# Four accumulator banks in turn for the mLSTM projections and gate tiles, and two accumulators for the modulation sums, in a one-core hybrid layer kernel

## The chip, the cores and the metric

The kernel runs on one core of a Trainium2 chip. The metric is the device time in microseconds from launch to end. TensorE does the matrix products and writes into PSUM, which has eight banks of 128 x 512 float32; VectorE (DVE), ScalarE (ACT) and GpSimd (POOL) do the elementwise work, and SyncE (SP), ScalarE and GpSimd issue DMA transfers. A PSUM bank can be given to a new product only when everything that reads the old one is done.

## The reference

One layer over 1024 latent tokens and 256 context tokens, width 1024. Cut to what matters:

```
u    = x * (1 + scale) + shift                       # latent; the context tokens likewise
p    = u @ w_in + b_in                               # 9280 columns, cut into q, k, v, gates ...
q, k = silu(short_conv(concat(q_m, k_m), conv_qk))   # mLSTM, 8 heads of 128: taps t-1, t, t+1
h_m  = mLSTM scan, both directions                   # chunked, with log-sum-exp gates
h_g  = gated linear attention (GLA), 4 heads, both directions
mix  = (sigmoid(gate_a) * (norm(h_m) * sigmoid(o_m)) @ w_branch_mlstm
        + sigmoid(gate_b) * (norm(h_g) * silu(z_g)) @ w_branch_gla) @ w_out
h    = layer_norm(ALPHA * h + g1 * mix)
h    = layer_norm(ALPHA * h + g2 * conv_glu(h * (1 + sc2) + sh2))
```

The vectors shift, scale, g1, sh2, sc2 and g2 are `silu(c) @ w_mod + b_mod`, 6144 columns. The first 2048 are made at the start; the other 4096 are made beside the GLA branch projection.

## The kernel before

Every large product is done as three products of rounded float32 halves (`mm3`, lines 279 to 285: high by high on L283, high by low on L284, low by high on L285). A **block** is one output tile of 128 x 512: 8 steps over the inner dimension by 3 products, so 24 matmuls into one PSUM bank. A block over the 256 context tokens has 24 matmuls of half the width.

**PSUM** is one pool with four tags of two banks each: `pj`, `pa`, `po` and `pt`. A tile of a tag takes one of its two banks as soon as that bank's last reader is done.

**The order on each engine** is not the order of the program text. A planner takes the instructions with their place in the text as their priority and lays out a fixed list for each engine, by its own costs; an instruction whose bank or buffer it holds to be taken yields to a later one. So the lists of TensorE, VectorE, ScalarE, GpSimd and the DMA queues are fixed when the kernel is made, and on the chip each engine goes through its list in order, with waits.

**The mLSTM stage.** For each head h, in the order of the text: the projections of q and k of head h+1 (`ml_proj_qk`, five blocks: two for q over the latent tokens, called q0 and q1 here, and three for k, called k0, k1 and the short k2 over the context); for every second head the projection of v for two heads (`ml_proj_v`, 240 half-width matmuls, always in `pj`); the last transposes of the head before (`late`, L844, evacuated by ScalarE on L845); the scan of head h (`ml_scan`); and one or two gate tiles (`fill`, `gate_tile`, two blocks each). TensorE fills the pauses of the scan with blocks of gate tiles. All blocks of q, k and the gate tiles lie in `pj`.

A block of q or k is read from its bank by one ScalarE instruction (L732) and by two to four VectorE instructions after it (the taps on L727, a one-column copy on L737, and edge columns). A gate tile's block is read by one ScalarE instruction (L537), which then goes out by a DMA of ScalarE's queue.

Inside `ml_scan`, GpSimd issues the loads of the decay tiles (L760, L761 and L764), ScalarE takes exponentials of them (L765, L769), and the products of k and q (L786, two tiles of four chunks) lie in `pa`. The GLA scan's last outputs lie in `pa` too, two tiles that are read on L690.

**The GLA branch stage.** For each of eight column blocks j of the branch output: `mod_sum(j)` adds up eight slices of `w_mod`, scaled by silu(c), into an accumulator on VectorE (L908), after a memset on GpSimd (L901) and a small DMA of the bias (L903). Four loads of 512 KB feed it through two buffers (L906). Then come two blocks of the branch product (mm3 on L956, banks `pj`, `pa`, `po` in turn), each scaled by a gate tile that is loaded (L953), passed through tanh (L954), multiplied (L957) and stored (L958). Then `mod_row(j)` sums the accumulator over its 128 partitions with a matmul (L913), copies the row (L914) and stores it (L915). All eight accumulators are the same buffer, `u19`.

Of the kernel before, what the change touches and what calls it, by code (L numbers as in the profile page):

```python
# [15 lines left out]
P = 128  # L16
# [20 lines left out]
def layer_kernel(ctx, tc, I, out, dbg=None):  # L37
# [16 lines left out]
    def nm(s):  # L54
        cnt[0] += 1
        return f"{s}_{cnt[0]}"

    def pt(tag, shape):
        return ps.tile(shape, F32, tag=tag, name=nm(tag))
# [17 lines left out]
    def ubt(i, shape, dt=F32):  # L77
        return ub.tile(shape, dt, tag=f"u{i}", name=nm(f"u{i}"))
# [35 lines left out]
    for l in range(7):  # L114
        h = 1 << l
# [47 lines left out]
    for k in range(KD):  # L163
        for hf in range(2):
            w = ubt(2 * k + hf, [P, 1024])
# [28 lines left out]
    for k in range(KD):  # L194
# [3 lines left out]
        for i in range(2):  # L198
            w = wm[2 * k + 1][:, 512:1024]
# [7 lines left out]
    for i in range(2):  # L207
        hi = stg.tile([P, 2, 256], F32R, tag="whi", name=nm("whi"), bufs=6)
        lo = stg.tile([P, 2, 256], F32R, tag="wlo", name=nm("wlo"), bufs=6)
        h, l = (t[:].rearrange("p a (b c) -> p (a b) c", c=P) for t in (hi, lo))  # L210
# [99 lines left out]
    def u_blk(b):  # L310
        if b < 2:
            return lambda k: (uh[k][:, b * 512:b * 512 + 512], ul[k][:, b * 512:b * 512 + 512])
        return lambda k: (cuh[k // 4][:, k % 4, :], cul[k // 4][:, k % 4, :])
# [9 lines left out]
    def proj(w, c, b, tag="pj"):  # L323
        p = pt(tag, [P, 512])
        mm3(p[:, 0:BW[b]], lambda k: w(k, c, P), u_blk(b))
        return p
# [68 lines left out]
    p = proj(w0, P, 2)  # L395
# [6 lines left out]
    for d, n in enumerate(("gla_gate_w_fwd", "gla_gate_w_bwd")):  # L402
# [4 lines left out]
        w = slot(10 + d, [96, SEQ], F32R)[:, 0:512]  # L407
# [121 lines left out]
            parts.append((hi, lo))  # L529
        return lambda k, c, n: tuple(t[:, k % 4, c:c + n] for t in parts[k // 4])  # L530

    def gate_tile(dst, off, cb0, j):
        w = wtile(w_in, off + j * P)
        for b in range(2):
            p = proj(w, 0, b)
            t = sc.tile([P, 512], F32, tag="gt", name=nm("gt"), bufs=2)
            A.activation(t[:], p[:], AF.Identity, scale=0.5, bias=cB(cb0 + j))  # L537
            A.dma_start(dst[j][:, b * 512:b * 512 + 512], t[:])
# [178 lines left out]
    def ml_proj_qk(h):  # L717
        w = wload([(w_in, O_QM + h * P, P, 0), (w_in, O_KM + h * P, P, P)])
        res = []
        for i in range(2):  # L720
            n = SEQ if i == 0 else L
            y = slot((0, 4)[h % 2] + i, [P, n])
            t0, t1, t2 = (cB(c_cv + 16 * j + 8 * i + h) for j in range(3))
            bs, b0, b2 = (cvb[:, j, 8 * i + h:8 * i + h + 1] for j in range(3))

            def tap(o, src, t):
                V.scalar_tensor_tensor(y[:, o:o + src.shape[1]], src, t, y[:, o:o + src.shape[1]],  # L727
                                       op0=ALU.mult, op1=ALU.add)
            for b in range(2 + i):
                m, o = BW[b], b * 512  # L730
                p = proj(w, i * P, b)
                A.activation(y[:, o:o + m], p[:, 0:m], AF.Identity, scale=t1, bias=bs)  # L732
                tap(o + 1, p[:, 0:m - 1], t0)
                tap(o, p[:, 1:m], t2)
                if b == 0:
                    ed = sc.tile([P, 1], F32, tag="ed", name=nm("ed"), bufs=2)
                    V.tensor_copy(ed[:], p[:, m - 1:m])  # L737
                if b == 1:
                    tap(o, ed[:], t0)
                    tap(o - 1, p[:, 0:1], t2)  # L740

                if b != 1:
                    V.tensor_tensor(y[:, o:o + 1], y[:, o:o + 1], b0, op=ALU.subtract)  # L743
                if b != 0:
                    V.tensor_tensor(y[:, o + m - 1:o + m], y[:, o + m - 1:o + m], b2, op=ALU.subtract)
            th = slot(15, [P, n])
            A.activation(th[:], y[:], AF.Tanh, scale=1.0 / QS if i == 0 else 1.0)
            V.scalar_tensor_tensor(y[:], th[:], 1.0, y[:], op0=ALU.add, op1=ALU.mult)
            res.append(y)
        return res  # L750
# [104 lines left out]

    gates = [(thb_d, O_GB, c_gb, j) for j in range(8)] + [(tha_d, O_GA, c_ga, j) for j in range(8)]

    def fill(n):
        for _ in range(n):
            gate_tile(*gates.pop(0))  # L860

    for h in range(GH):
        q, k = gla_qk(h) if h else (q0, k0)
# [13 lines left out]
    for h in range(MH):  # L877
        nxt = ml_proj_qk(h + 1) if h + 1 < MH else None
        if h and h % 2 == 0:
            v2 = ml_proj_v(h // 2)  # L880
        late()
        rest.append(ml_scan(h, *qk, v2[h % 2]))
        qk = nxt
        fill(2 if h < 2 or h > 5 else 1)
    late()
    while gates:
        fill(1)
# [4 lines left out]
    tags = ("pj", "pa", "po")  # L892
# [4 lines left out]
        return tags[seq[0] % 3]  # L897

    def mod_sum(b):
        acc = ubt(19, [P, 512])  # L900
        G.memset(acc[:], 0.0)  # L901
        c0 = 2048 + b * 512
        SY.dma_start(acc[0:1, :], I["b_mod"][c0:c0 + 512].unsqueeze(0))  # L903
        for k2 in range(0, KD, 2):
            raw = ubt((16, 18)[k2 // 2 % 2], [P, 2, 512])
            SY.dma_start(raw[:], I["w_mod"][k2 * P:(k2 + 2) * P, c0:c0 + 512].rearrange("(k p) c -> p k c", p=P))  # L906
            for i in range(2):
                V.scalar_tensor_tensor(acc[:], raw[:, i, :], sC[:, k2 + i, 0:1], acc[:], op0=ALU.mult, op1=ALU.add)  # L908
        return acc

    def mod_row(b, acc):
        p = pt("pt", [P, 512])
        T.matmul(p[0:1, :], ones[:], acc[:], start=True, stop=True)  # L913
        V.tensor_copy(acc[0:1, :], p[0:1, :])  # L914
        SY.dma_start(md_d[b * 512:b * 512 + 512].unsqueeze(0), acc[0:1, :])  # L915

    def gated(off, cb0, src_d, silu):
        hi, lo = [], []
        for j2 in range(4):
            w = wload([(w_in, off + j2 * 256, 256, 0)])  # L920
            for e in range(2):
                j = 2 * j2 + e
                hi.append(slot(j, [P, SEQ], F32R))
                lo.append(slot(8 + j, [P, SEQ], F32R))
                hr = ubt(16 + j % 2, [P, SEQ])
                SY.dma_start(hr[:], src_d[j][:])
                ht = ubt(18, [P, SEQ])
                zz2 = ubt(19, [P, 2, 512]) if silu else None
                for b in range(2):
                    s_ = slice(b * 512, b * 512 + 512)  # L930
                    p = proj(w, e * P, b, ytag())
                    th = sc.tile([P, 512], F32, tag="gt", name=nm("gt"), bufs=2)
                    A.activation(th[:], p[:], AF.Tanh, scale=0.5, bias=cB(cb0 + j))
                    hs = hr[:, s_]
                    if silu:
                        zt = zz2[:, b, :]
                        A.activation(zt, p[:], AF.Identity, scale=0.5, bias=cB(cb0 + j))
                        V.tensor_tensor(hs, zt, hs, op=ALU.mult)
                    V.scalar_tensor_tensor(ht[:, s_], th[:], 1.0, hs, op0=ALU.add, op1=ALU.mult)
                    split(hi[j][:, s_], lo[j][:, s_], ht[:, s_])  # L940
        return hi, lo

    ya_d = [drt(f"ya{j}", [P, SEQ]) for j in range(8)]
    ghi_, glo_ = gated(O_ZG, c_zg, hg_d, True)
    for j2 in range(4):
        w = wload([(I["w_branch_gla"], j2 * 256, 256, 0)])
        for e in range(2):
            j = 2 * j2 + e
            acc = mod_sum(j)
            for b in range(2):  # L950
                s_ = slice(b * 512, b * 512 + 512)
                th = sc.tile([P, 512], F32, tag="gt", name=nm("gt"), bufs=2)
                SY.dma_start(th[:], thb_d[j][:, s_])  # L953
                A.activation(th[:], th[:], AF.Tanh)  # L954
                p = pt(ytag(), [P, 512])
                mm3(p[:], lambda k: w(k, e * P, P), lambda k: (ghi_[k][:, s_], glo_[k][:, s_]))  # L956
                V.scalar_tensor_tensor(th[:], th[:], 1.0, p[:], op0=ALU.add, op1=ALU.mult)  # L957
                SY.dma_start(ya_d[j][:, s_], th[:])  # L958
            mod_row(j, acc)

    rowF = ubt(19, [P, 3, P])
    cw = [I["ffn_conv_w"][a, b] for a in range(3) for b in range(3)]
# [18 lines left out]
    for j2 in range(4):  # L981
        w = wload([(I["w_branch_mlstm"], j2 * 256, 256, 0)])
        for e in range(2):
            j = 2 * j2 + e
# [4 lines left out]
            for b in range(2):  # L989
# [4 lines left out]
                p = pt(ytag(), [P, 512])  # L994
# [110 lines left out]
    for f in range(NF):  # L1105
        w = wload([(I["w_up"], f * P, P, 0), (I["w_up"], D_FF + f * P, P, P)])
# [6 lines left out]
        for b in range(2):  # L1113
            for e, (dst, bi) in enumerate(((gf, f), (val, NF + f))):
                p = pt("pj", [P, 512])
# [16 lines left out]
        acc = fp.tile([P, ROWS, GRID_W], F32, tag="acc", name=nm("acc"), bufs=2)  # L1132
# [78 lines left out]
    for i, (g, cb_, k) in enumerate(main):  # L1211
        k0, k1 = ((0, N_RES), (N_RES, NF))[g]
        s_ = slice(cb_ * 512, cb_ * 512 + 512)
        if k == k0:
            acc = [pt(b, [P, 512]) for b in bt]
# [31 lines left out]
    for j, c in enumerate(todo[len(main):]):  # L1247
        if j >= 6:
            if j < 10:
                h = (ubt(10 + j - 6, [P, 2, 512], F32R) if j < 8 else  # L1250
                     fin.tile([P, 2, 512], F32R, tag="gl", name=nm("wlate"), bufs=2))
                h = [h[:, 0, :], h[:, 1, :]]
            else:
                h = [fin.tile([P, 512], F32R, tag="z1", name=nm("wlate"), bufs=4)[:] for _ in range(2)]
# [3 lines left out]
    for t in range(8):  # L1258
        for cb_ in (1,):
            p = pt(("pj", "pa", "po", "pt")[t % 4], [P, 512])  # L1260
# [3 lines left out]
        n = nt[t]  # L1264
# [30 lines left out]
```

## Time and profile before

| | |
|---|---|
| time, median of 3 runs (lowest, highest) | 2317.84 us (2316.33, 2319.12) |
| the profiled execution: its own time | 2320.08 us |
| its span, first to last instruction | 2318.3 us |
| mean granted TensorE clock over the span | 0.991 |
| TensorE busy | 2241.0 us, 97% |
| VectorE busy | 1323.9 us, 57% |
| ScalarE busy | 728.3 us, 31% |
| GpSimd busy | 253.9 us, 11% |

A busy time counts instructions that overlap once. The ends of matmuls are modelled in such a profile, so the start of one matmul to the start of the next tells more than the length of one. A wait is put down to the instruction that last raised the semaphore; where that instruction does not touch the thing waited for, it is a neighbour of the one that does.

### The profile page before, as it was taken

What the parts mean: (1) busy time and instruction counts of PE and PEld (TensorE: products, weight loads), DVE (VectorE), ACT (ScalarE), POOL (GpSimd) and SP (SyncE); (2) the same over time, 40 slices, a digit from 0 to 9 for tenths busy, and PEclk for the clock granted to TensorE, in tenths of its full rate; (3) what the DMA queues carried; (4) which work ended last, traced back from release to release, by engine and by line L of the source; (5) the groups of instructions that cost most, each with busy time, mean ns of one, the idle gap of its engine ahead of it and who ended that gap; (6) DMA issues with size and microseconds to landing.
All of it is one profiled execution on the core that took longest, in us unless ns stands there. A gap on an engine that the chain in (4) does not pass through costs nothing.

```text
span 2318.3 us, 30341 instructions
## 1 busy us (share of the span) xinstructions
PE 2241.0 (97%) x11641; PEld 1881.1 (81%) x11641; DVE 1323.9 (57%) x2511; ACT 728.3 (31%) x1239; POOL 253.9 (11%) x254
## 2 busy tenths in 40 slices
PE   8989999998999999999999999999999999999998
PEld 4979898987888888897876788787788888888886
DVE  6485737376563665656345543477856556554257
ACT  3563323224323331322432133312433333333110
POOL 1010101011110111101110032101210000000100
PEclk9999999999999999999999999999999999999999
DMA  8231121104332433324346645524411222225721
GB/s 284 67 118 51 59 69 44 60 26 106 98 100 57 116 97 97 104 64 119 100 145 219 209 130 159 179 81 143 130 37 55 62 66 77 75 92 188 219 77 73
DMA packets 187747, 246.56 MB, mean 106 GB/s; under 512 B 16257, under 2 KB 129537, under 8 KB 187601
## 3 DMA queue, kind: packets, MB, share of 16 engines
q1 hardware_dynamic: 164673, 179.16, 24.5%
q0 software_dynamic: 12416, 44.21, 7.2%
q10 hardware_dynamic: 10512, 21.24, 2.5%
q8 instruction: 92, 1.51, 0.3%
q14 instruction: 54, 0.44, 0.1%
HBM read 186.57 MB, written 49.60 MB: 102 GB/s over the span
## 4 chain that ended last, share of the span: by engine, by line
PE 76%; DMA 8%; issue 6%; DVE 6%; ACT 2%; POOL 1%; SPq 0%; DVEq 0%; POOLq 0%; ACTq 0%
PE pj L283 15%; PE pj L284 15%; PE pj L285 15%; DMA qq<-re 2%; DMA u<-in_w_mod_dram 2%; PE pa L618 2%; PE po L284 2%; PE po L283 2%; PE po L285 2%; PE pa L285 2%; PE pa L284 2%; PE pa L283 2%; DMA s<-rr 1%; PE pt L796 1%; PE po L816 1%
## 5 line engine op out<-in xcount | busy, mean ns | idle before, releaser
L283 PE MATMUL pj<-u,whi 128*128 128x512 f32 (+1 forms) x816 | 315.8, 387 | 17.0 <-DVE s L743 5.7
L253 DVE TENSOR_TENSOR wlo<-raw,whi 128x512 fp32r<-128x512 f32 x302 | 218.0, 726 | 167.2 <-ACT whi L252 163.2
L284 PE MATMUL pj<-u,whi 128*128 128x512 f32 (+1 forms) x816 | 313.0, 384 | 0.0
L285 PE MATMUL pj<-u,wlo 128*128 128x512 f32 (+1 forms) x816 | 312.8, 384 | 0.0
L252 ACT ACTIVATE whi<-raw 128x512 fp32r<-128x512 f32 x302 | 188.8, 629 | 385.2 <-PE pj L285 155.2
L285 PE MATMUL pj<-s,wlo 128*128 128x512 f32 x784 | 305.7, 390 | 2.0 <-DVE wlo L253 2.0
L283 PE MATMUL pj<-s,whi 128*128 128x512 f32 x784 | 305.4, 390 | 0.4 <-ACT val L1118 0.4
L284 PE MATMUL pj<-s,whi 128*128 128x512 f32 x744 | 290.4, 390 | 3.0 <-POOL s L1086 3.0
L1142 DVE SCALAR_TENSOR_TENSOR acc<-g,colF,acc 128x945 f32<-128x945 f32 (+2 forms) x168 | 206.4, 1229 | 139.8 <-ACT acc L1133 137.8
L283 PEld LDWEIGHTS pj<-u,whi 128*128 128x128 f32 x816 | 155.2, 190 | 47.9 <-ACT s L769 11.1
L283 PE MATMUL pj<-whi,u 128*128 128x256 f32 x640 | 181.7, 284 | 0.0
L285 PE MATMUL pj<-whi,u 128*128 128x256 f32 x640 | 181.4, 283 | 0.0
L284 PE MATMUL pj<-wlo,u 128*128 128x256 f32 x640 | 181.4, 283 | 0.0
L285 PEld LDWEIGHTS pj<-u,wlo 128*128 128x128 f32 x816 | 155.2, 190 | 26.5
L284 PEld LDWEIGHTS pj<-u,whi 128*128 128x128 f32 x816 | 155.3, 190 | 25.7
L285 PEld LDWEIGHTS pj<-s,wlo 128*128 128x128 f32 x784 | 147.2, 188 | 33.2 <-DVE wlo L253 2.7
L283 PEld LDWEIGHTS pj<-s,whi 128*128 128x128 f32 x784 | 147.2, 188 | 32.0 <-ACT val L1118 0.8
L284 PEld LDWEIGHTS pj<-s,whi 128*128 128x128 f32 x744 | 139.7, 188 | 34.4 <-POOL s L1086 4.3
L283 PEld LDWEIGHTS pj<-whi,u 128*128 128x128 f32 x640 | 122.8, 192 | 0.5
L284 PEld LDWEIGHTS pj<-wlo,u 128*128 128x128 f32 x640 | 122.8, 192 | 0.0
L285 PEld LDWEIGHTS pj<-whi,u 128*128 128x128 f32 x640 | 122.8, 192 | 0.0
L727 DVE SCALAR_TENSOR_TENSOR s<-pj,colB,s 128x511 f32<-128x511 f32 (+2 forms) x96 | 57.5, 613 | 85.1 <-ACT s L732 84.2
(496 smaller groups left out, 4044.1 us busy)
## 6 DMA issues: line engine op xcount, KB each, us to landing
u<-in_w_mod_dram SPq DMA_DIRECT2D x48, 512.0 KB
raw<-in_w_in_dram SPq DMA_DIRECT2D x96, 256.0 KB
raw<-in_w_up_dram SPq DMA_DIRECT2D x176, 128.0 KB
raw<-in_w_in_dram SPq DMA_DIRECT2D x96, 128.0 KB
raw<-in_w_down_dram SPq DMA_DIRECT2D x44, 256.0 KB
s<-rmask POOLq DMA_DIRECT2D x16, 512.0 KB, 4.9
s<-rr POOLq DMA_DIRECT2D x16, 512.0 KB, 7.9
qq<-re POOLq DMA_DIRECT2D x16, 512.0 KB, 6.5
```

The lines of the kernel that those rows point to most:

```text
L252: A.activation(hi, src, AF.Copy)
L253: eng.tensor_tensor(lo, src, hi.bitcast(F32), op=ALU.subtract)
L283: T.matmul(p, lh, rh, start=k == 0, stop=False)
L284: T.matmul(p, lh, rl, start=False, stop=False)
L285: T.matmul(p, ll, rh, start=False, stop=k == nk - 1)
L618: T.matmul(p[:, c, :], kc[:, o:o + P], pairs(qq, 1, hs, o, 64 // hs), start=True, stop=True)
L727: V.scalar_tensor_tensor(y[:, o:o + src.shape[1]], src, t, y[:, o:o + src.shape[1]], op0=ALU.mult, op1=ALU.add)
L796: T.matmul(p[:, i, :], kt[d][:, c, :], v[:, c, :], start=True, stop=True)
L816: T.matmul(p[:, i, :], dt_[d][:, c, :], v[:, c, :], start=True, stop=False)
L1142: V.scalar_tensor_tensor(av, g[:, r0 + dy:r1 + dy, c0 + dx:c1 + dx], convw(3 * ky + kx, f), av, op0=ALU.mult, op1=ALU.add)
```

## The change

The projections of q and k take `pj` and `pa` in turn, by the sum of the part and the block: q0 `pj`, q1 `pa`, k0 `pa`, k1 `pj`, k2 `pa`. The gate tiles of the mLSTM heads take `pj` for the first block and `pa` for the second; the gate tiles of the GLA heads stay in `pj`. The modulation sums take two accumulators, `u17` and `u19`, in turn, and the row of sum j-1 is made after the blocks of column block j instead of the row of sum j; the row of the last sum follows at the end. No arithmetic is added or removed.

```diff
-    def gate_tile(dst, off, cb0, j):
+    def gate_tile(dst, off, cb0, j, tags=("pj", "pj")):
         w = wtile(w_in, off + j * P)
         for b in range(2):
-            p = proj(w, 0, b)
+            p = proj(w, 0, b, tags[b])
...
-                p = proj(w, i * P, b)
+                p = proj(w, i * P, b, ("pj", "pa")[(i + b) % 2])
...
-    def fill(n):
+    def fill(n, tags=("pj", "pj")):
         for _ in range(n):
-            gate_tile(*gates.pop(0))
+            gate_tile(*gates.pop(0), tags)
...
-        fill(2 if h < 2 or h > 5 else 1)
+        fill(2 if h < 2 or h > 5 else 1, ("pj", "pa"))
...
     def mod_sum(b):
-        acc = ubt(19, [P, 512])
+        acc = ubt((17, 19)[b % 2], [P, 512])
...
+    accs = {}
     for j2 in range(4):
...
-            acc = mod_sum(j)
+            accs[j] = mod_sum(j)
...
-            mod_row(j, acc)
+            if j:
+                mod_row(j - 1, accs[j - 1])
+    mod_row(7, accs[7])
```

## Rows read from the trace of the kernel before

**Rows 1.** The page, its first section: busy time, share, instructions of each engine.

```profile
PE 2241.0 (97%) x11641; PEld 1881.1 (81%) x11641; DVE 1323.9 (57%) x2511; ACT 728.3 (31%) x1239; POOL 253.9 (11%) x254
```

**Rows 2.** Who TensorE waited for, whole span: us in total, times, longest.

```profile
PE pj L283 <- DVE s L743: 5.7, 3, 2.8
...
PE pt L913 <- DVE u L908: 4.4, 4, 1.8
PE pj L283 <- ACT gt L537: 4.3, 2, 2.3
PE pj L283 <- DVE s L727: 4.3, 3, 1.7
PE pt L913 <- issue: 4.1, 2, 2.2
...
PE pj L283 <- DVE ed L737: 1.6, 1, 1.6
```

**Rows 3.** By stretch: us, busy (x) of five engines, granted clock, DMA share, GB/s.

```profile
636.95:640.36 3.41, 3.41 (x10) 2.67 (x9) 1.88 (x3) 2.68 (x7) 1.17 (x1) 0.50 0.22 81
...
1110.00:1195.00 85.00, 85.00 (x377) 70.41 (x376) 31.70 (x45) 36.91 (x60) 19.06 (x15) 1.00 0.30 94
...
1195.30:1300.70 105.40, 98.25 (x395) 73.94 (x394) 55.02 (x79) 21.50 (x35) 4.51 (x8) 0.97 0.70 227
```

**Rows 4.** TensorE in order of time, around one wait: start, us, instruction, idle before.

```profile
925.70 0.39 PE L284 MATMUL pj<-u,whi 128*128 128x512 f32 x1
925.93 0.39 PE L285 MATMUL pj<-u,wlo 128*128 128x512 f32 x1
928.94 0.47 PE L283 MATMUL pj<-u,whi 128*128 128x512 f32 x1 [2.62 <-DVE s L743]
...
942.82 1.03 PE L844 MATMUL pt<-ident,s 128*128 128x128 f32 x8
943.69 0.83 PE L786 MATMUL pa<-s,s 128*128 128x128 f32 x6
```

**Rows 5.** ScalarE in order of time, same stretch.

```profile
920.85 1.06 ACT L765 ACTIVATE qq<-qq 128x1024 f32<-128x1024 f32 x1 [4.39 <-DMA qq<-re]
924.26 2.16 ACT L769 ACTIVATE s<-s,ta 128x128 f32<-128x128 f32 x7 [2.35 <-DMA s<-rr]
926.32 0.76 ACT L732 ACTIVATE s<-pj,cvb,colB 128x512 f32<-128x512 f32 x1
...
930.89 0.76 ACT L732 ACTIVATE s<-pj,cvb,colB 128x512 f32<-128x512 f32 x1
...
940.82 2.71 ACT L252 ACTIVATE whi<-raw 128x512 fp32r<-128x512 f32 x4
```

**Rows 6.** VectorE in order of time, same stretch.

```profile
928.64 0.15 DVE L737 COPY ed<-pj 128x1 f32<-128x1 f32 x1
```

**Rows 7.** TensorE in order of time, inside the first stretch of rows 3.

```profile
637.23 0.63 PE L283 MATMUL pj<-u,whi 128*128 128x512 f32 x1
637.65 0.63 PE L284 MATMUL pj<-u,whi 128*128 128x512 f32 x1
```

**Rows 8.** TensorE, GpSimd, SyncE, VectorE in order of time: one accumulator's round.

```profile
1212.65 1.02 PE L913 MATMUL pt<-u,ones 128*1 128x512 f32 x2 [1.88 <-issue]
...
1217.45 0.52 POOL L901 MEMSET u<- 128x512 f32 x1 [16.90 <-DMA md_d<-u]
...
1219.88 0.26 SPq L903 DMA_DIRECT2D u<-in_b_mod_dram  x1
...
1223.03 0.74 DVE L908 SCALAR_TENSOR_TENSOR u<-u,sC,u 128x512 f32<-128x512 f32 x1
...
1234.35 1.86 PE L913 MATMUL pt<-u,ones 128*1 128x512 f32 x2 [2.22 <-issue]
```

**Rows 9.** VectorE in order of time: the GLA scan's last outputs leaving `pa`.

```profile
507.19 1.26 DVE L690 TENSOR_SCALAR hn<-pa,gss 128x256 f32<-128x256 f32 x3
...
566.74 0.47 DVE L690 TENSOR_SCALAR hn<-pa,gss 128x256 f32<-128x256 f32 x1
```

## Prediction

> **What bounds the kernel now.** I read the page first. TensorE is busy for 2241.0 of 2318.3 us [rows 1]; no other engine comes near. With one engine so full, a change that adds no arithmetic can only save what TensorE waits, and what its clock loses after a wait. So the second view is who TensorE waited for [rows 2], and the third its clock by stretch [rows 3].
>
> The waits are short, and the two edited places hold many of them. Blocks of the mLSTM projections and gate tiles (L283 into `pj`) waited 5.7 + 4.3 + 4.3 + 1.6 = 15.9 us, in nine waits; the row of the modulation sum (L913) waited 4.4 + 4.1 = 8.5 us, in six [rows 2].
>
> Are the first waits for a bank? One of them [rows 4]: the products that end a block are issued at 925.70 and 925.93, the next block's first at 928.94. The same weights feed both blocks, so they are not missing. The instruction named (L743) does not touch PSUM; its neighbour does, the copy on L737, the last reader of block q0's bank, which ends at 928.64 + 0.15 = 928.79 [rows 6]. ScalarE explains why it is late: it takes its list in order, and L765 and L769 wait there for the decay tiles' DMAs, 4.39 and 2.35 us [rows 5]; q0's evacuation (L732) stands behind them and starts at 926.32. With two banks of `pj`, the third block finds q0 still unread. It is a wait for a bank, set by a DMA.
>
> The clock adds to it. After four of the waits the granted clock was 0.50 for 3.4 us; one stands in rows 3. There matmuls start 637.65 - 637.23 = 0.42 us apart [rows 7], otherwise 0.23 [rows 4]: the lower of the two levels, 1.2 GHz. Each such stretch costs 3.41 x (1 - 0.23/0.42) = 1.5 us. Two of the four follow a projection's wait, two a row's.
>
> **Part 1: the projections and gate tiles.** It adds no instruction, no DMA and no evacuation. At 0.23 us per matmul a block takes 24 x 0.23 = 5.5 us. With banks `pj`, `pa`, `pa`, `pj`, `pa` a replay of that stretch [rows 4 to 6] runs so. k0 is wanted at 926.2 and takes the `pa` bank that the gate tile before left free; k1 follows at 931.7 in the other `pj` bank, k2 at 937.2 in the bank of q1. q1 is read by the L732 at 930.89, and its VectorE readers need about what q0's took, 928.79 - 926.32 = 2.5 us, so it is free at 933.4, 3.8 us early. The bank wait of 2.62 us goes.
>
> Gained: all but the 1.6 us at the first head, 14.3 us, and two half-clock stretches, 3.0 us. I leave out the 1.6 us because there both `pa` banks still hold the GLA scan's last outputs: three of their four readers run at 507.19, the fourth not before 566.74 [rows 9], and k0 must let it go first. Between nothing and a wait of one block (5.5 us) I take no change there.
>
> What is late next: the product of k and q (L786), which needs both `pa` banks and comes right after k2. Its second tile wants the bank of k2. TensorE ends k2 at 937.2 + 2.8 (half a block) = 940.0; the transposes (L844) take 943.69 - 942.82 = 0.9 us [rows 4], and the first products of L786 about 0.8, so the second tile is wanted at 941.7. k2's evacuation on ScalarE stands behind k1's (0.76) and four weight splits (2.71) [rows 5], so k2 is read from about 937.2 + 0.8 + 2.7 = 940.7, and VectorE's taps end some 2.3 us on (under q0's 2.5, as the block is shorter): 943.0. A wait of 1.3 us. Only the scans with no v projection between k2 and L786 have it, heads 1, 3 and 5: 3.9 us. For the others 240 half-width matmuls cover it. If that cover is thin, the same 1.3 us stands at more heads; queued behind a waiting L786 on TensorE is the whole scan.
>
> Part 1: 14.3 + 3.0 - 3.9 = 13.4 us; from 18.9 (no new wait, the first head too) down to 9.5 (the new wait twice as long).
>
> **Part 2: the sums.** The number of L913, L914, L915 and memsets stays at eight each. The round of one accumulator [rows 8]: row at 1212.65, its DMA lands and the memset runs at 1217.45, the bias DMA is issued at 1219.88 (SP's list holds other transfers ahead of it), the first sum runs at 1223.03, and the next row starts at 1234.35 after a wait of 2.22 us. That is 21.7 us a round, and TensorE has two blocks of its own in it, 11.0 us, and one row, 1.0; the planner filled the rest with later blocks, which are no loss, and the wait is the loss. With two accumulators a round may take two column blocks, about 24 us: 2.3 us to spare for every row but the last. The last follows the one before with no column block between, and I leave its wait as large as the largest today, 2.2 us.
>
> L914 on VectorE and L915 on SP move by one column block, past two loads L953, two stores L958, the w_mod loads and the bias of the next sum; on POOL the next memset waits for that L915 as it does today. I cost the move at nothing: the spare 2.3 us hides it, and without that each row costs what L915 is late. u17 was the buffer into which the next stage loaded one head output early; that load now comes after the sums. TensorE can run several blocks ahead there, so nothing; at worst one load of 512 KB.
>
> The stage runs faster, and that has a price. A column block moves 4 x 512 KB of w_mod, 512 KB of gate tiles in, 512 KB out and 512 KB of weights: 3.67 MB. The stretch of the branch products ran at 227 GB/s with a DMA share of 0.70 [rows 3], so at a full share 227/0.70 = 324 GB/s, or 11.3 us for it, against 12.0 us of TensorE. That is tight. Between no wait and all of the gain I take 0.4 us a column block, 3 us.
>
> Part 2: 8.5 + 3.0 - 2.2 - 3.0 = 6.3 us; from 11.5 down to 0.
>
> **The sum.** 13.4 + 6.3 = 19.7 us off the profiled execution's own 2320.08 is 2300.4. That execution stands 2.2 us above the median of the runs, so 2317.84 - 19.7 = 2298 us. The case's own range is 18.9 + 11.5 = 30.4 down to 9.5 us: 2287 to 2308.
>
> **The rivals.**
> *A, the branch stage becomes bound by DMA.* If the share tops out below 0.94 (11.3/12.0), the rows or the gate tiles wait for transfers and part 2 gives nothing. For it: 0.70 is a mean over uneven demand, and SP issues in order. Against it: later blocks can fill. 2317.8 - 13.4 = 2304.
>
> *B, the evacuation catches up.* The 14.3 us of part 1 come back as waits at L786, and only its clock (3.0) and part 2 are left: 2317.8 - 9.3 = 2308. For it: VectorE and ScalarE do the same work after the same DMA. Against it: they sit idle before it [rows 5], and four heads have the v projection as cover.
>
> *C, slower: a head's scan held at L786.* The scan's `pa` tiles now queue behind blocks that ScalarE reads in order, and a block can lie there while L765 and L769 wait for a DMA: 4.39 + 2.35 = 6.7 us [rows 5]. If the planner's new list puts such a block ahead of L786, eight heads at up to 6.7 us lose 54. It decides from 19.7/8 = 2.5 us a head; at half of the 54 the time is 2317.8 - 19.7 + 27 = 2325. Against it: the DMAs wait for the scan that has just ended, and the projections come between.
>
> *D, no change.* The planner lays all lists anew; the waits sum up elsewhere as fast as they go here: 2318.
>
> *E, slower by the clock.* Each change of bank could let TensorE pause and drop its clock. One half-clock stretch costs 1.5 us; two more at each of eight heads, 24 us, and part 1 gone: 2317.8 - 6.3 + 24 = 2335. Against it: from 1110 to 1195 us blocks already go round `pj`, `pa` and `po`, and TensorE was busy for 85.00 of 85.00 us at a granted clock of 1.00 [rows 3]. The Trainium skill warns of this (TensorE: Matmul & The Clock Gate, A second HAM failure mode: psum-queue depth-cycling): cycling PSUM through its banks made TensorE idle briefly between groups of products, and its clock went to and fro between its levels. By that rule E would be the forecast; the trace does not agree, in the stretch just named.
>
> **How the numbers follow.** Forecast 0.58, A 0.15, B 0.07, C 0.10, D 0.08, E 0.02. About 0.2% (4.6 us) is what a measurement of this kernel can tell from no change, so faster is below 2313.2. The forecast, A and B lie there: 0.80. D: 0.08. C and E: 0.12. The range takes in A, B and D, leaves out C and E above, and goes 2 us below the best case for waits not counted here: 2285 to 2318.
>
> **What would show it.** In the view of TensorE's waits, L283 into `pj` and `pa` behind L743, L727 and L537 should fall from 15.9 to 3 us or less, and L913 from 8.5 to about 2. L786 should appear with about 4 us. The half-clock stretches near 637, 791, 1214 and 1234 should be gone. The eight L913 should stand some 12 us apart at first, not 21.7, and the stage's DMA rate should rise from 227 towards 300 GB/s. The forecast is wrong if L786 waits over 2.5 us a head, if waits on whi, gt or po grow in the branch stage, or if the rows wait as long as before.

## The result and the profile after

The changed kernel takes 2295.83 us (median of four runs, 2294.39 to 2298.17); the kernel before, beside it on the same chip, 2317.09 us. The ratio is 0.9912, 95% interval 0.9895 to 0.9929. Timed again it was 0.9906 (0.9892 to 0.9920). So the change saves some 21 us; the prediction was 2298, faster. The profiled execution took 2294.39 us, with a span of 2292.6.

The page's busy line of the changed kernel, which answers to [rows 1]:

```profile
PE 2235.5 (98%) x11641; PEld 1881.5 (82%) x11641; DVE 1321.3 (58%) x2511; ACT 728.8 (32%) x1239; POOL 253.3 (11%) x254
```

The same 11,641 matmuls in a span 25.7 us shorter: nothing was taken off any engine, only idle time and slow clock. Who TensorE waited for in the changed kernel, which answers to [rows 2] (us in total, times, longest; below L944 the line numbers are up to 3 higher than before):

```profile
PE pt L777 <- ACT s L845: 5.8, 1, 5.8
PE pj L283 <- ACT whi L252: 4.8, 1, 4.8
...
PE pt L501 <- DVE ta L502: 3.2, 1, 3.2
...
PE pt L913 <- DVE u L908: 2.4, 3, 1.4
PE pa L283 <- DVE s L727: 2.2, 1, 2.2
```

The blocks' 15.9 us of [rows 2] have become one wait of 2.2 us, and the rows' 8.5 us have become 2.4. L786 is not in the view at all. New is a single wait of 4.8 us for `whi`, a set of weights. Three stretches of the changed kernel (us, busy of five engines, granted clock, DMA share, GB/s), which answer to [rows 3]:

```profile
1110.00:1195.00 85.00, 85.00 (x374) 70.06 (x374) 36.85 (x51) 34.72 (x57) 19.19 (x16) 1.00 0.42 126
...
1177.00:1283.70 106.70, 100.29 (x411) 74.20 (x409) 67.92 (x99) 19.12 (x32) 5.49 (x9) 1.00 0.80 253
...
1284.48:1287.89 3.41, 3.41 (x8) 2.70 (x9) 3.19 (x5) 0.00 (x0) 0.00 (x0) 0.50 0.91 255
```

The branch stage now moves 253 GB/s at a share of 0.80, against 227 at 0.70. The eight rows, 19 us apart on the mean before, follow 12.3 to 13.7 us apart. The last line is the clock's answer to the new wait: 3.41 us at 0.50, the lower level, 1.2 GHz.

To put the gain in its places I cut each execution at three instructions that every kernel has: the first L447 (a memset where the mLSTM gates begin), the last transpose L844 (of the last head) and the first L997 (where the second branch is first added to the first). Of the changed kernel, from the view of a line, with the first and last start:

```profile
L844 PE MATMUL pt<-ident,s x64: 271/272/273, 651.8 to 1089.8; 128*128 128x128 f32 x64
...
L1000 DVE TENSOR_TENSOR u<-gt,u x16: 686/693/694, 1378.7 to 1462.4; 128x512 f32<-128x512 f32 x16
```

and of the kernel before:

```profile
L844 PE MATMUL pt<-ident,s x64: 271/272/273, 657.2 to 1108.1; 128*128 128x128 f32 x64
...
L997 DVE TENSOR_TENSOR u<-gt,u x16: 686/693/694, 1399.8 to 1483.5; 128x512 f32<-128x512 f32 x16
```

L447 starts at 486.4 before and at 484.6 after, 1.8 us apart ahead of any edit. The table calls the three stretches heads (first L447 to last L844), branches (to the first L997) and rest (to the last L1266, which is L1269 after). The heads went from 621.7 to 605.2 us (-16.5), the branches from 291.7 to 288.9 (-2.8), the rest, in which nothing was edited, from 911.0 to 906.4 (-4.6). With the 1.8 that is 25.7 us between the two profiled executions; between the medians it is 21.3, since the one before (2320.08 us) stood 3.0 us above the 2317.09 and the one after 1.4 below its median. All kernels of this study, cut in the same way (us, one profiled execution each; the ratio is that of the timed runs):

| kernel | heads | branches | rest | ratio to before, 95% |
|---|---|---|---|---|
| before | 621.7 | 291.7 | 911.0 | 1 |
| changed | 605.2 | 288.9 | 906.4 | 0.9912 (0.9895 to 0.9929) |
| changed, again | 606.3 | 288.0 | 907.9 | 0.9906 (0.9892 to 0.9920) |
| banks alone | 605.8 | 295.0 | 907.0 | 0.9910 (0.9897 to 0.9923) |
| banks alone, again | 605.3 | 295.4 | 907.2 | 0.9923 (0.9909 to 0.9938) |
| q and k banks alone | 606.5 | 296.7 | 907.0 | 0.9907 (0.9894 to 0.9920) |
| gate tiles' banks alone | 623.5 | 288.9 | 910.5 | 0.9989 (0.9980 to 0.9999) |
| sums alone | 628.0 | 285.9 | 909.3 | 0.9990 (0.9979 to 1.0001) |
| two banks, VectorE empties | 611.2 | 288.9 | 907.5 | 0.9944 (0.9931 to 0.9956) |
| changed, loads by GpSimd | 603.3 | 303.8 | 907.4 | 0.9968 (0.9954 to 0.9982) |
| changed, gate tile moved | 595.4 | 288.1 | 908.0 | 0.9858 (0.9845 to 0.9870) |
| ... and weights by ScalarE | 595.3 | 290.7 | 907.3 | 0.9854 (0.9837 to 0.9871) |
| ... and three load slots | 595.3 | 279.7 | 906.3 | 0.9821 (0.9804 to 0.9839) |
| banks alone, three slots, one sum | 605.8 | 287.2 | 906.7 | 0.9903 (0.9880 to 0.9926) |

A stretch is that of one execution, and a difference of a few us between two of them need not be the edit's: in the heads of the kernel with the sums alone nothing is edited and the instructions stand in the same order on every engine as before, and they took 6.3 us longer.

### The profile page after: what moved, and what is told of

Read it like the earlier page. It is cut to its first block, busy times and chain, and to the rows that moved or that the text cites. A ratio compares the mean times of both kernels' runs of the same rounds, so it can differ in the third digit from the quotient of the medians.

```text
span 2292.6 us, 30337 instructions
## 1 busy us (share of the span) xinstructions
PE 2235.5 (98%) x11641; PEld 1881.5 (82%) x11641; DVE 1321.3 (58%) x2511; ACT 728.8 (32%) x1239; POOL 253.3 (11%) x254
## 5 line engine op out<-in xcount | busy, mean ns | idle before, releaser
L253 DVE TENSOR_TENSOR wlo<-raw,whi 128x512 fp32r<-128x512 f32 x302 | 216.2, 721 | 166.8 <-ACT whi L252 162.0
L283 PE MATMUL pj<-s,whi 128*128 128x512 f32 x784 | 305.6, 390 | 0.3 <-ACT val L1121 0.3
L283 PE MATMUL pj<-u,whi 128*128 128x512 f32 (+1 forms) x528 | 207.1, 392 | 4.8 <-ACT whi L252 4.8
L285 PE MATMUL pj<-u,wlo 128*128 128x512 f32 (+1 forms) x528 | 206.2, 391 | 0.0
L284 PE MATMUL pj<-u,whi 128*128 128x512 f32 (+1 forms) x528 | 205.9, 390 | 0.0
L283 PE MATMUL pj<-whi,u 128*128 128x256 f32 x640 | 181.5, 284 | 0.0
L283 PEld LDWEIGHTS pj<-s,whi 128*128 128x128 f32 x784 | 147.2, 188 | 33.3 <-issue 1.7
L283 PE MATMUL pa<-u,whi 128*128 128x512 f32 (+1 forms) x376 | 142.1, 378 | 2.2 <-DVE s L727 2.2
L284 PE MATMUL pa<-u,whi 128*128 128x512 f32 (+1 forms) x376 | 141.9, 377 | 0.0
L285 PE MATMUL pa<-u,wlo 128*128 128x512 f32 (+1 forms) x376 | 141.2, 376 | 0.0
L283 PEld LDWEIGHTS pj<-whi,u 128*128 128x128 f32 x640 | 122.8, 192 | 0.1
L283 PEld LDWEIGHTS pj<-u,whi 128*128 128x128 f32 x528 | 100.2, 190 | 24.1 <-ACT whi L252 5.2
```

The costliest lines, as they stand in the source:

```text
L253: eng.tensor_tensor(lo, src, hi.bitcast(F32), op=ALU.subtract)
L283: T.matmul(p, lh, rh, start=k == 0, stop=False)
L284: T.matmul(p, lh, rl, start=False, stop=False)
L285: T.matmul(p, ll, rh, start=False, stop=k == nk - 1)
```

## The experiments

My theory after the result: the banks gave nearly everything; of the two accumulators little is left, since the stage runs into a new wait for weights. The rival: the sums gave a good part, and the early difference is spread.

### The change in its parts

Four kernels have parts of the change. The banks alone:

```diff
-                p = proj(w, i * P, b)
+                p = proj(w, i * P, b, ("pj", "pa")[(i + b) % 2])
...
-        fill(2 if h < 2 or h > 5 else 1)
+        fill(2 if h < 2 or h > 5 else 1, ("pj", "pa"))
```

> The kernel before with the banks alone: q and k projections and gate tiles of the mLSTM heads through pj and pa in turn, the sums of the branch stage as before. Theory: the mLSTM part of the changed kernel gave about 16.5 us by the trace (18.3 us at the last L844 less 1.8 us that the two executions differ ahead of any edit), and the branch stage only about 2.8, so this alone gives 16.5: about 2300.5 us, L283 waits of later heads gone, L913 rows as before. Rival (the gain came from the two sum accumulators, and the early mLSTM difference is spread): about 2315.

Measured 2298.85 us, 0.9910: 20.9 us. The heads' stretch is that of the changed kernel (605.8), while the branches' grew from 291.7 to 295.0, and the rows wait 11.9 us in this kernel against 8.5 before: some 3 us of what the heads gain are waited away there. So the two parts interact, and the prediction had no term for it.

The sums alone:

```diff
-        acc = ubt(19, [P, 512])
+        acc = ubt((17, 19)[b % 2], [P, 512])
...
-            mod_row(j, acc)
+            if j:
+                mod_row(j - 1, accs[j - 1])
```

> The kernel before with the two sum accumulators alone. Theory: the rows' 8.5 us of waits shrink to about 2.5, but the weights of the next stage come late (the new wait of 4.8 us on whi with a 3.41 us half-clock stretch behind it), so the net gain is about 3 us (1 to 6): about 2314, rows some 12 us apart instead of 21.7. Rival 1 (the prediction's own term: nothing is late behind it): 6.3 to 8.5 us, about 2309. Rival 2 (the branch stage is bound by its transfers): within 1 us of no change.

Measured 2317.56 us, 0.9990 (0.9979 to 1.0001): 2.3 us, at most 4.9. The rows waited for nothing any more, and the branches' stretch is 285.9, but the new wait for `whi` is there, 4.4 us with a half-clock stretch of 3.41 us behind it. The number is the theory's, but its account is not shown: the branches gave 5.8 us with that wait in them, and the heads took 6.3 us longer, with two more stretches of 3.41 us at 0.50 and 1.7 us more of L283's waits, though their lists are those of the kernel before. The twelve runs have a mean granted clock of 0.990, the 23 of the kernel before beside them 0.992, so it is hardly chance of this one execution; why is open. For the sums by themselves 6.3 us and more are excluded, in the kernel's time.

Of the banks, the q and k projections alone (only the first pair of lines of the banks' diff):

> Of the banks, the q and k projections alone; gate tiles stay in the two pj banks. Theory: what TensorE waited for in a head is that k's third block needs the bank of q's or k's earlier block, which ScalarE empties late, and the gate tiles come into the stalls only as the next in line; so this alone gives nearly all, 13 to 16.5 us: about 2302. Rival: the gate tiles' own banks carry half (the gt waits of 4.3 us stay and the stall slips on into them): 6 to 9 us, about 2309.

Measured 2298.78 us, 0.9907, the whole gain of the banks. The gate tiles alone (only the other pair and `tags[b]` in `gate_tile`):

> Of the banks, the gate tiles alone (pj, pa); q and k stay in the two pj banks. Theory: 0 to 4 us, about 2315, since the q and k blocks still wait for one another's bank and only the gt waits (4.3 us) can go. Rival: 8 us or more, about 2309, as the gate tiles no longer hold a pj bank when the next q block comes.

Measured 2316.83 us, 0.9989: 2.5 us. TensorE's waits of this kernel say why so little:

```profile
PE pj L283 <- DVE s L743: 13.2, 6, 3.5
...
PE pj L283 <- DVE s L727: 4.1, 2, 2.6
```

The waits behind `gt` (4.3 us in [rows 2]) are gone, and those behind L743 rose from 5.7 to 13.2. A gate tile in another bank reaches the next q block sooner, and the wait for q's bank is longer by as much. A stall that sits on a chain has to be cut where the bank is held, not where the queue stands.

### Is the bank late because ScalarE is late?

Two banks as before, but VectorE is the first reader of each block, with the same arithmetic:

```diff
-                A.activation(y[:, o:o + m], p[:, 0:m], AF.Identity, scale=t1, bias=bs)
+                V.tensor_scalar(y[:, o:o + m], p[:, 0:m], t1, bs, op0=ALU.mult, op1=ALU.add)
...
-            A.activation(t[:], p[:], AF.Identity, scale=0.5, bias=cB(cb0 + j))
+            V.tensor_scalar(t[:], p[:], 0.5, cB(cb0 + j), op0=ALU.mult, op1=ALU.add)
```

> The kernel before with its two pj banks, but the first reader of each q and k block (L732) and of each gate tile (L537) is VectorE instead of ScalarE, with the same arithmetic. Theory (the banks come free late because ScalarE reaches its evacuation late: its list is in order and holds decay-tile work and waits ahead of it): the waits at L283 behind L743, L727 and gt shrink from 15.9 us to under 5 with two banks still, and the time falls by 8 to 16 us, to about 2308. Rival (two banks are too few whoever empties them; VectorE has three more readers per block and about 0.7 us more for each of 40 plus 24 blocks, 44 us in all): the waits stay or grow, 2318 to 2335.

Measured 2305.69 us, 0.9944: 13 us without a third bank. L283's waits behind L743, L727 and L537 are one view line now, behind the last of VectorE's readers:

```profile
PE pj L283 <- DVE ed L737: 9.5, 4, 3.2
```

The time is inside the forecast, the waits are not (9.5 us where under 5 was expected). And not all of the 13 us are the banks'. The edit reaches the gate tiles of the GLA heads too, and in the GLA scan, ahead of the heads, a wait of TensorE is shorter. Before:

```profile
PE pa L618 <- DVE qq L626: 8.3, 13, 1.6
```

and in this kernel:

```profile
PE pa L618 <- DVE qq L626: 4.6, 11, 1.0
```

In the heads it gave 10.5 us, where four banks give about 16, and of the 15.9 us of waits 6.4 are gone. So ScalarE's list, held by the decay tiles' DMAs, is a part of the cause, and two banks are short by themselves for the rest. Two more banks hide both at no work.

### Why are the weights late after the branch stage?

SyncE's queue of the changed kernel in that corner, from the view of waits between 1240 and 1292 us:

```profile
SPq L906 <- DVE u L908: 17.3, 14, 2.0
```

SyncE takes its list in order and stands at the loads of `w_mod` (L906), which wait for VectorE to free one of two slots; the weights of the next stage (L263) are behind them. (It also stands for 7.2 us at the stores of L959 there.) Three kernels try to get them past. First, the loads of `w_mod` off that list, on GpSimd's:

```diff
-            SY.dma_start(raw[:], I["w_mod"]...)
+            G.dma_start(raw[:], I["w_mod"]...)
```

> The changed kernel with the loads of w_mod in the branch stage (L906, 32 of them) issued from GpSimd's queue instead of SyncE's. Theory: the changed kernel's new wait of 4.80 us for whi at 1284.46 comes from SyncE's order, as its list stood 17.3 us in L906 waiting for slots between 1240 and 1292 while the next stage's weights (L263) were behind it; off that list the weights come in time, the wait and its 3.41 us half-clock stretch (1.7 us) go, 4 to 7 us less than the changed kernel, about 2291. Rival (the DMA engines, 0.80 busy in that stretch, are the limit): the weights are as late, within 2 us of the changed kernel. Rival 2 (GpSimd's own list delays the sums, whose memset stands between): rows wait again, 3 us or more slower.

Measured 2312.16 us, 0.9968: 15 us slower than the changed kernel. The wait for `whi` is indeed gone. TensorE reaches those weights later in this kernel, but they do come early: their loads now wait for a free buffer (SyncE's waits from 1160 to 1300 us):

```profile
SPq L263 <- DVE wlo L253: 45.8, 18, 15.5
```

So SyncE's order held them back. But the rows wait 16.1 us:

```profile
PE pt L913 <- DVE u L908: 16.1, 5, 7.8
```

The sums are late for their loads. VectorE waited for `w_mod` in the changed kernel and in this one, between 1160 and 1300 us:

```profile
DVE u L908 <- DMA u<-in_w_mod_dram: 23.6, 20, 2.7
```

```profile
DVE u L908 <- DMA u<-in_w_mod_dram: 44.1, 26, 3.5
```

With two slots a sum goes load, add, free the slot, load, so that the time of a load stands in each round. An issue takes 0.72 us on GpSimd and 0.38 on SyncE, and a load lands 5.1 us after it on GpSimd's queue. For SyncE's the page shows no landing; where VectorE stood idle for a load, the sum began 4.8 us after the issue there (median in the changed kernel), and 5.3 us after it on GpSimd's. By an estimate from these figures four loads through two slots, each with two sums of 0.74 us [rows 8], take about 2 x (5.1 + 1.5) = 13 us; the rows of this kernel stand 12 to 16 us apart. What share the other transfers have, which SyncE now issues unhindered, was not taken apart. So the theory was right on the cause and wrong on the time, and what happened is what rival 2 expected of the rows, by another route than its memset.

The Trainium skill (DMA: Bandwidth & Descriptors, Issuing engines are not separate DMA queues) says that transfers issued by several engines run on the same DMA engines, and that spreading the issue saves only the time of issuing, usually small. Here moving the loads cost 15 us, where by that rule it should have made little difference. Whether the order of the transfers, the longer issue or GpSimd's queue itself made the loss, no run here separates.

Second, on the changed kernel with one gate tile moved (below), only the four late weight loads go to ScalarE's queue:

```diff
-            w = wload([(w_in, off + j2 * 256, 256, 0)])
+            w = wload([(w_in, off + j2 * 256, 256, 0)], q=SY if silu or j2 else A)
```

> The changed kernel with the gate tile moved behind head 6 (0.9858 of before), and the first four weight loads of the stage after the branch stage (L263 of the O_OM weights) issued from ScalarE's queue instead of SyncE's. Theory (those weights are late because SyncE's list holds them behind loads of w_mod that wait for a slot): the wait for whi, 4.1 us there and 4.8 in the changed kernel, falls under 1 us and its half-clock stretch of 6.83 us (3.4 us lost) goes, while the rows keep waiting under 2.5 us: 4 to 7 us less, about 0.9833 of before. Rival (ScalarE, which has to wait for a free raw slot when it issues, holds up its own conversions and tanh): the wait moves to other weights or to gt, and nothing is won.

Measured 2285.93 us, 0.9854, the same as without it (0.9858). The wait for `whi` went from 4.1 us to nothing, and the rows' wait rose from 0.8 to 8.5:

```profile
PE pt L913 <- DVE u L908: 8.5, 3, 4.2
```

The theory had the cause of the weights' lateness right and what follows wrong: the weights came early and the sums late (VectorE waits 29.8 us for `w_mod`, against 24.8 without the edit). So far the limit could still be the transfers themselves (share 0.80). Third, again with the gate tile moved, a slot more, so that a load can run ahead; the two sums share one slot, in halves:

```diff
-        acc = ubt((17, 19)[b % 2], [P, 512])
+        acc = acc2[:, b % 2, :]
...
-            raw = ubt((16, 18)[k2 // 2 % 2], [P, 2, 512])
+            raw = ubt(16 + (4 * b + k2 // 2) % 3, [P, 2, 512])
...
+    acc2 = ubt(19, [P, 2, 512])
```

> The changed kernel with the gate tile moved behind head 6, and both sums in the two halves of one scratch slot, so that the loads of w_mod turn through three slots (16, 17, 18) instead of two. Theory: SyncE waits for VectorE to free a slot 17.3 us between 1240 and 1292 in the changed kernel; a third slot lets a load run ahead, that wait falls by more than half, the weights come in time, and the rows wait no more: 4 to 7 us less than 0.9858 of before. Rival 1 (the transfers are the limit at 0.80 busy): within 2 us. Rival 2 (the two sums share a tile, so that one is held until the other's row is out): rows wait again, 3 us or more slower.

Measured 2276.7 us, 0.9821. By the ratios that is 8.6 us less than without it, more than forecast, and 41 us less than the kernel before: of all kernels here the fastest. The branch stretch of this kernel:

```profile
1160.00:1275.00 115.00, 115.00 (x475) 85.92 (x474) 77.44 (x113) 27.26 (x44) 8.04 (x11) 1.00 0.82 266
```

TensorE is busy for all of 115 us; no row and no weight waits, and the clock stays at 1.00. VectorE waits 9.0 us for `w_mod` here instead of 24.8, while SyncE's own wait for a slot fell only from 17.6 to 10.7 us (in the 52 us that end just behind the last row), less than the half that was forecast. At 266 GB/s the transfers are not the limit: what held the sums back was the time of a load, with two slots to hide it.

Is then the second accumulator needed? The banks alone, three slots, one accumulator (only the middle pair of the last diff):

> The banks alone, with the loads of w_mod in three slots (16, 17, 18) and still one sum accumulator, as before the change. Theory (two causes in series: the accumulator holds a sum back until the row before is out, the slots hold the loads back): the rows stay about 19 us apart and go on waiting 6 us or more, the stretch from the last L844 to the first L997 stays within 4 us of the banks alone (295.0 and 295.4), 0.990 to 0.992 of before. Rival (only the loads' slots limited the sums, and the second accumulator was beside the point): rows about 12 us apart, the stretch about 283, 0.9865.

Measured 2293.89 us, 0.9903 (0.9880 to 0.9926), rows 15 to 18 us apart, the branches' stretch 287.2 us against 295.2 for the banks alone. The time is what the theory said, the rows and the stretch lie between the two theories: the slot alone gives 8.0 us of that stretch, the second accumulator alone 6.8 (288.5 for the changed kernel's two), both together 15.5 (279.7, with the gate tile moved as well). So the two gains add up, and neither stands behind the other. That is by stretches of one or two executions; by the times the slot alone is worth some 3 us (0.9903 against 0.9917), which the intervals do not tell from nothing.

### The last head's wait

The largest wait of the changed kernel is the 5.8 us at L777, which the edit did not touch. One gate tile is moved from behind head 1 to behind head 6:

```diff
-        fill(2 if h < 2 or h > 5 else 1, ("pj", "pa"))
+        fill((2, 1, 1, 1, 1, 1, 3, 2)[h], ("pj", "pa"))
```

> The changed kernel with one gate tile moved from behind head 1 to behind head 6 (counts 2,1,1,1,1,1,3,2). Theory: the last head's wait at L777 (5.8 us, and 6.83 us at half clock behind it, 3.4 us) is a lack of other work for TensorE, and a gate tile of 48 products (about 10.6 us) placed there covers it: 5 to 9 us less than the changed kernel, about 2290; head 1 has no wait that needs its second tile. Rival 1 (the planner places it elsewhere, or the gates come too late for the last head): no change. Rival 2 (head 1 needs it): a stall of some us opens at head 2, and nothing is won.

Measured 2285.02 us, 0.9858, against 0.9906 for the changed kernel on the same chip: 11 to 12 us less, more than forecast. TensorE's waits no longer list L777. From the first head to the end of the branch stage the clock stays at its upper level, 2.4 GHz:

```profile
545.00:1271.00 726.00, 721.25 (x4098) 620.91 (x4096) 419.08 (x1121) 232.11 (x450) 97.89 (x89) 1.00 0.42 122
```

### The parts once more

The changed kernel and the banks alone, each timed again:

> The changed kernel as it is, timed beside the next three on one chip. 0.9905 of before, about 2297 us: the banks alone gave 21 us of 2320 in the first comparison, and the sums alone 2.4 (0 to 5), so that the two together should be 0.990 to 0.991.

> The banks alone once more. In the first comparison the banks alone stood at 0.991 of before, and the changed kernel at 0.9912 and 0.9906, so that by the times the two accumulators are worth 0 to 2.4 us beside the banks, where two traces of the stretch from the last L844 to the branch stage's end give 6.1 us (295.0 against 288.9). If the stretch tells it, this stands at 0.993; if the times do, at 0.991.

Measured 0.9906 and 0.9923. By the times the accumulators are worth some 2 us beside the banks (0.9909 against 0.9917, mean of two each), by the stretch 6.8. The intervals are some 3 us wide on each side, and a stretch is one execution. What they are worth is not settled closer than that.

## Why the prediction held, and where its terms were off

**The bank wait** was read rightly. 15.9 us of L283 became 2.2, against 3 or less, and what is left is at the first head, as said: 553.19 us, waiting for VectorE's L727. The first head lost something besides: its L501 waits 3.2 us instead of 1.8, in every kernel with q and k in four banks. That ScalarE's list makes the bank late is shown in part: where VectorE empties the banks, 9.5 us of the waits are left.

**The clock.** The stretches near 637, 791, 1214 and 1234 us are gone, as said. Two new ones came, 3.41 us each, at 554.03 behind the first head's wait and at 1284.48 behind `whi`, which the sum didn't have.

**The new wait at L786** is the step that failed: 3.9 us charged, none seen. Of head 5 in the changed kernel, in order of time (start, us, instruction):

```profile
925.63 0.28 PE L285 MATMUL pa<-u,wlo 128*128 128x256 f32 x1
925.75 1.03 PE L844 MATMUL pt<-ident,s 128*128 128x128 f32 x8
926.63 0.83 PE L786 MATMUL pa<-s,s 128*128 128x128 f32 x6
927.55 0.44 PE L777 MATMUL pt<-ident,s 128*128 128x128 f32 x2
927.83 0.39 PE L786 MATMUL pa<-s,s 128*128 128x128 f32 x2
927.97 0.48 PE L283 MATMUL pj<-u,whi 128*128 128x512 f32 x1
928.28 0.60 PE L777 MATMUL pt<-ident,s 128*128 128x128 f32 x4
928.64 0.47 PE L284 MATMUL pj<-u,whi 128*128 128x512 f32 x1
928.95 0.66 PE L786 MATMUL pa<-s,s 128*128 128x128 f32 x4
```

and VectorE's readers of k2 in the same place:

```profile
927.49 0.48 DVE L727 SCALAR_TENSOR_TENSOR s<-pa,colB,s 128x255 f32<-128x255 f32 x1
...
928.37 0.47 DVE L727 SCALAR_TENSOR_TENSOR s<-pa,colB,s 128x255 f32<-128x255 f32 x1
```

k2's last product starts at 925.63, and VectorE's L727 on its bank ends at 928.84, 3.0 us after the block's end: what the prediction worked out (940.0 to 943.0). But TensorE wanted the second tile at 928.95, 3.2 us on, where it counted 1.7. Between the starts of the two tiles the planner put six matmuls of L777 and two of a gate tile. The demand was wrong, not the supply. In the trace before, L777's matmuls stand among L786's in the same way (at 944.61 and 945.34), so that this could have been read there. In heads 1 and 3 the second tile starts 2.3 us behind the first as well (652.66 and 654.99, 795.09 and 797.42).

The count was wrong too: head 0's scan has no v projection between k2 and L786 either (k2's last product is at 590.60, the first of L786 at 591.38), so by the prediction's own rule four heads would have waited, 5.2 us, and only three, not four, have that cover.

**Part 1's size.** Predicted 13.4, range to 18.9; the heads' stretch gave 16.5 in the changed kernel and 15.9 to 16.4 with the banks alone. 13.2 of the 16.5 are TensorE's waits in that stretch (24.9 to 11.7 us), the rest clock and pitch. Without the 3.9 the sum would have been 17.3. The times give the banks 18 to 21 us; in the profiled executions 4 us lie besides in a stage that no edit touches, and some 3 us are lost in the rows' longer waits.

**Part 2's size.** Predicted 6.3, from nothing to 11.5. Alone 2.3 us (nothing to 4.9), beside the banks 2 by the times and 6.8 by the stretch. The rows did as said: 8.5 us to 2.4, 12.3 to 13.7 us apart (the 21.7 of the prediction was the longest round before, the mean was 19). What failed is the step that costs the moved work and the fuller stage: the contention was charged to the rows, 0.4 us each, at a share that would rise to 300 GB/s. It came out as one wait of 4.8 us for the next stage's weights on SyncE's list, with its clock, at 253 GB/s. What stands behind the row's moved work on SyncE's list was costed at nothing; there L263 stood behind L906. The prediction named waits on `whi` as a sign against itself, and had no price for them.

**The sum** came within 2 us of the medians (21.3 against 19.7), and in part that is luck. By stage the two misses have opposite signs: 3.1 us too little for the heads and 3.5 us too much for the branches, with 6.4 us of untouched stretches on top, most of which the medians do not show. By part of the change the stretches come nearer: the banks alone give about 16 us in the heads and lose 3.5 in the branches, 12.6 against 13.4, and the accumulators beside them 6.8 against 6.3. But there too a charge that never came, the 3.9 us at L786, stands in for losses that the sum did not have: the rows' longer wait behind faster heads, the wait for `whi`, and two half-clock stretches. By the times the split is another again (18 to 21 and 2).

**The rivals.** A (bound by DMA): no; the kernel with three slots moves 266 GB/s in that stage and waits for nothing, though what A expects, a stage that gives little, is what the times show. B and C: no L786 waits. D: the gain stands in the kernels with the part alone. E: from 543 to 1048 us, heads in four banks in turn, TensorE was busy for 500.03 of 505.00 us at a granted clock of 1.00:

```profile
543.00:1048.00 505.00, 500.03 (x3084) 444.44 (x3082) 293.09 (x887) 165.76 (x335) 71.16 (x65) 1.00 0.37 102
```

and before, with two banks, for 490.86 of 507.00 at 0.99:

```profile
543.00:1050.00 507.00, 490.86 (x3017) 434.05 (x3017) 289.79 (x861) 158.43 (x317) 64.83 (x59) 0.99 0.34 94
```

By the rule of the Trainium skill that the prediction weighed (TensorE: Matmul & The Clock Gate, A second HAM failure mode: psum-queue depth-cycling) that stretch should have gone to and fro; it did not: the only drop that begins in it is the one at 554.03, behind a wait of 2.2 us.

## What to carry to other kernels

A wait for a bank is shortened by emptying it earlier (here from 15.9 to 9.5 us) and cured by having another bank while it is read (2.2 us left); the second costs no engine anything, and an idle bank of another tag serves. Move the block that holds the bank, not the one that stands in the queue behind it. Before giving a stage a second accumulator, look whether its loads have enough slots to run ahead, and what is behind them in the issuing queue: here, by the stretches, a slot was worth about as much as the accumulator, and only both together made the stage wait for nothing.

## What the chip showed that was not expected

A stage that no edit touches takes 909.3 to 911.0 us in the three kernels in which q and k stay in two banks emptied by ScalarE, and 906.3 to 908.0 in the eleven other profiles. The order of instructions by line on TensorE, VectorE, ScalarE and GpSimd is the same there before and after. Of the 4.6 us between before and after, 2.5 begin at a load on GpSimd that waits for a store to land, before and after:

```profile
1606.85 0.53 POOL L1131 DMA_DIRECT2D u<-n  x1 [4.43 <-DMA y<-u]
```

```profile
1583.50 0.53 POOL L1134 DMA_DIRECT2D u<-n  x1 [2.69 <-DMA y<-u]
```

From there VectorE is late, and TensorE of the kernel before waits 2.0 us for it behind L253, which the changed kernel does not. Another 1.6 us come near the end, where the kernel before waits 1.1 us at L1185 and L1186 for a set of weights. Why the store lands later is open.

Nor does the granted clock answer to a wait by its length alone. In the changed kernel the wait of 4.80 us for `whi` was followed by 3.41 us at 0.50; in the kernel with the gate tile moved the same wait, 4.13 us there, by 6.83 us. With three slots the clock stands at 1.00 for 1720 us on end, a stretch in which no wait of TensorE is over 1.4 us:

```profile
544.00:2264.00 1720.00, 1711.92 (x8476) 1435.72 (x8474) 983.51 (x1889) 525.16 (x862) 197.47 (x175) 1.00 0.38 115
```
